# Turning the delta rule's normalized outputs by VectorE blocks and DRAM instead of TensorE

## The chip, the cores and the metric

The program runs on one core of one Trainium2 chip. The metric is the device time of one execution in microseconds (us); below it the median of several runs is given, and one execution was also taken by the hardware profiler.

## What is computed

One layer of a hybrid decoder trunk on 2048 tokens of width 1024, preceded by 16 meta tokens, in float32. The input is RMS-normalized and multiplied by one wide matrix; its columns feed two groups. Group A is a gated DeltaNet of 8 heads of 128 channels; group B is a short gated convolution. Both are put side by side, multiplied by `w_out`, added to the input and normalized once more.

```python
h = rmsnorm(x, norm_g); p = h @ w_in
q, k, v = split(silu(causal_dwconv(p_qkv, dn_conv_w)))        # l2norm of q and k per head
def step(S, inp):                                             # per head, chunk after chunk
    v_new = u_c - w_c @ S
    o = qd_c @ S + qk_c @ v_new
    S = S * gl_c + kd_c.T @ v_new
    return S, o
o = rmsnorm(o, dn_out_g) * silu(dn_z)                         # per head of 128 channels
o_sc = sc_b * causal_dwconv(sc_c * sc_h, sc_conv_w) * silu(sc_z)
return rmsnorm(x + concat([o_dn, o_sc]) @ w_out, final_g)
```

The part that matters here is the last line but two: the scan leaves `o` with tokens on the partitions, the norm is taken along the channels, and the product with `w_out` wants channels on the partitions. So each piece of 128 tokens by 128 channels has to be turned.

## The kernel before, in words

The 2048 tokens go through in two halves of 1024 (`hf`). For each half the wide product runs as a list of jobs of 128 columns each, and each job in groups of up to 512 tokens. A float32 product is made of three passes with rounded parts (`hh`, `hl` of the activations, `wh`, `wl` of the weights): hh·wh, hl·wh and hh·wl, 24 matmuls to a group, into one of three PSUM buffers `mm`. ScalarE rounds a loaded weight tile `wr` to `wh`, VectorE makes `wl` of the difference (`split_w`, line 713), and only when the second half of `wl` is made is the next weight load issued into that buffer (`load_w`, line 707).

Beside this runs the delta rule of one head after another, 16 in all (8 heads in each half of the tokens), as generators that a planner (`Model`, `pump`) resumes between the matmuls. The planner keeps an estimate of each engine's time, and an operation is written into its engine's list when the estimate says that its inputs are there. So the order on TensorE (PE), VectorE (DVE), ScalarE (ACT) and GpSimd (POOL) is fixed when the program is built, and each of these engines works through its list in that order and waits where an input is late. All DMAs are issued by SyncE (SP), also in one fixed order; that order is set by a scheduler of the framework.

- `delta_front` (line 962) makes the masked products of a head and inverts its 32x32 blocks on VectorE by `substitution` (line 933): 31 pairs `prod`, `XT`. The blocks pass through DRAM on their way there (`nbd<-E`, then `nb<-nbd`), four small DMAs each way.
- `delta_back` (line 1110) merges the blocks, loads the decays `qd` from DRAM and turns keys, values and queries on TensorE (PSUM tag `ta`). `qd` has one buffer, which the scan reads up to its last chunk, so the load for the next head waits for TensorE.
- `delta_scan` (line 1290) goes through the 8 chunks of a head. For each chunk: TensorE makes `rec<-S,k`; VectorE makes `yy` from it; TensorE adds `o<-S,qd` to the output and makes `rec<-yy,W`; ScalarE makes `vn`; TensorE makes `rec<-vn,kd` and `o<-vn,P`; VectorE makes the next state `S`. After every 4 chunks ScalarE copies the outputs from PSUM `o` to `os`.
- `delta_out` (line 1340) takes each `os` (4 pieces of 128x128; 32 such outputs, two for each head). ScalarE sums the squares, GpSimd and VectorE make the scale `so`, VectorE multiplies `os` by it, TensorE turns the four pieces into PSUM (`rec<-ident,os`, lines 1363 to 1365), and VectorE multiplies them with the gain and the gate into `zs` (line 1369). A DMA stores `zs` to `mixd`, from which the last product loads its input.

In the text an output is named by its head (0 to 15) and by first or second half (`b4` 0 or 1). While the first half is being normalized and turned, the scan of the second four chunks goes on.

Line 118, which the profile gives for nearly all instructions, is the planner's helper; so the rows are told apart by tile names.

Of the kernel before, what the change touches and what calls it, by code (L numbers as in the profile page):

```python
# [29 lines left out]
class Model:  # L30
# [33 lines left out]
    def after(self, *aps, slot=None, eng=None, lag=0.0, least=0.02):  # L64

        t = self.free["PE"] + least
        for a in aps:
            t = max(t, self.ready.get(a.tensor.name, 0.0))
        if slot is not None:
            q = self.slots.get((id(slot[0]), slot[1]), ())  # L70
            if len(q) == self.bufs.get((id(slot[0]), slot[1])):
                t = max(t, self.used.get(q[0], 0.0))
        if eng is not None:
            t = max(t, self.free[eng] - lag)
        return t - self.free["PE"]
# [98 lines left out]
def hybrid_trunk(  # L174
# [22 lines left out]
    nbd = tc.dram_tile([2, 32, 32, 32], F32, name="nbd")  # L197
    xtd = tc.dram_tile([2, 32, 32, 32], F32, name="xtd")
    ged = tc.dram_tile([2, NH * 9, 128], F32, name="ged")
    nmd = tc.dram_tile([2, NM, NM], F32, name="nmd")  # L200
    gtd = tc.dram_tile([2, NH * 9, 128], F32, name="gtd")

# [110 lines left out]
    def vt(pool, shape, tag, **kw):  # L313
        t = pool.tile(shape, kw.pop("dt", F32), tag=tag, name=tag, **kw)
        return model.tile(pool, tag, kw.get("bufs", nbufs.get(id(pool), 1)), t)
# [202 lines left out]
    def normalize(i):  # L518

        xt = vt(dp, [128, NC, 128], "kd").rearrange("p c i -> p (c i)")  # L520
        nc.sync.dma_start(xt, xs[HALF + 128 * i :][:128])
        yield after(xt)
        st = statistics(xt, 128, vt(dp, [128, 1840], "gw", dt=BF16))
        gains = []
        yield from hold("Q", True)

        def gain(c2):
            gains.append(vt(dp, [128, NC, 64], "Q").rearrange("p c i -> p (c i)"))
            nc.sync.dma_start(gains[c2], norm_g[0, 512 * c2 : 512 * c2 + 512].partition_broadcast(128))

        gain(0)
        yield after(gains[0], st[1])
        rs = refine(st, 128)
        for c2 in range(2):
            xc = xt[:, 512 * c2 : 512 * c2 + 512]
            nc.vector.scalar_tensor_tensor(xc, xc, rs, gains[c2], op0=ALU.mult, op1=ALU.mult)
            if c2 == 0:
                gain(1)
                yield after(gains[1])
        held.discard("Q")  # L540
        nc.sync.dma_start(xnd[i], xt)
        done.add(("xn", i))
# [28 lines left out]
    def hold(tag="ta", keep=False):  # L571
# [3 lines left out]
        if keep:  # L575
            held.add(tag)

    G = {}

    def gates(hf):  # L580
# [18 lines left out]
        yield after(abT, slot=(pta, "ta"))  # L599
        yield from hold()  # L600
        pt = ptile(pta, "ta", [128, 512])
        gw = vt(dp, [128, 920], "gw")
        ab2 = gw[:, 0:288].rearrange("p (c m) -> p c m", m=32)
        for c in range(NC):
# [78 lines left out]
        yield 3.5  # L683
        nc.scalar.activation(gT[:Wd], gT[:Wd], AF.Exp)
        nc.sync.dma_start(ged[hf, :Wd], gT[:Wd])
        G[hf] = dict(beta=beta, gcum=gcum, neg=neg, nch=nch)
        yield 2.0
        done.add(("G", hf))
# [121 lines left out]
    slot = {}  # L810
# [529 lines left out]
    def delta_out():  # L1340

        for _ in range(4 * NH):
            while not outputs:
                yield 0.3
            i, b4, os_, sq = outputs[0]
            hf, hd = divmod(i, NH)
            cs = slice(4 * b4, 4 * b4 + 4)
            mo, so, py, ptm = (vt(dp, [128, 4], a) for a in ("mo", "so", "opy", "opt"))
            yield after(os_)
            for c in range(4):  # L1350
                nc.scalar.activation(junk[:, 0:128], os_[:, c, :], AF.Square, accum_out=mo[:, c : c + 1])
            yield after(mo, eng="DVE", lag=0.3)
            nc.vector.scalar_tensor_tensor(mo, mo, 1.0 / HD, sq[:, cs], op0=ALU.mult, op1=ALU.add)
            power(py, mo, 4)
            yield after(py, eng="DVE", lag=0.3)
            newton(so, mo, py, ptm)
            nc.vector.tensor_tensor(
                out=os_, in0=os_, in1=so.unsqueeze(2).to_broadcast([128, 4, 128]), op=ALU.mult
            )
            while ("z", i) not in done:  # L1360
                yield 0.3
            yield after(os_, slot=(prec, "rec"))
            pt = ptile(prec, "rec", [128, 4, 128])
            for c in range(4):
                tr(pt[:, c, :], os_[:, c, :])
            outputs.popleft()
            ms = slice(512 * b4, 512 * b4 + 512)
            zs = slot[i]["zs"]
            nc.vector.scalar_tensor_tensor(
                zs[:, ms], pt.rearrange("p c i -> p (c i)"), dng, zs[:, ms], op0=ALU.mult, op1=ALU.mult  # L1370
            )
            t0 = hf * NC + 4 * b4
            nc.sync.dma_start(
                mixd[t0 : t0 + 4, :, hd, :].rearrange("t p j -> p t j"),
                zs[:, ms].rearrange("p (t j) -> p t j", j=128),
            )
            if b4 == 1:
                done.add(("out", i))
            yield 0.3

    STEP = 1.0
    SUBST = 0.8
    BACKLOG = 3
# [253 lines left out]
```

## Time and profile before

| | |
|---|---|
| median of 3 runs | 2236.77 us (2235.26 to 2238.23) |
| the profiled execution, its own time | 2236.26 us |
| its span from first to last instruction | 2234.5 us |
| PE busy | 2174.5 us, 97% |
| DVE busy | 1451.7 us, 65% |
| ACT busy | 854.0 us, 38% |
| POOL busy | 189.3 us, 8% |
| packets of the DMA queue that SP feeds, share of 16 engines | 46.0% |

Busy time is time in which an instruction was running; overlapping ones count once. The time outside the span is 1.8 us. In the rows further down, the name of an instruction is out<-in by the program's tile names, "xN" is the number of instructions, and a bracket at the end of a row gives the idle time of the engine before it and what ended it.

### The profile page before, as it was taken

To read this page: it belongs to the slowest core of one execution; us is meant where nothing else is said; L and a number is where in the kernel's file an instruction comes from. 1 tells how busy PE (TensorE), PEld (TensorE's weight loads), DVE (VectorE), ACT (ScalarE), POOL (GpSimd) and SP (SyncE) were. 2 spreads that over 40 slices of the span, in tenths; PEclk is the share of its full clock that TensorE was granted. 3 is DMA by queue.
4 is the path that set the end of the run, shared out by engine and by line. 5 is a ranking of instruction groups with operands and counts; after the bars stand their busy time and mean duration, and the time that the engine had idled before them with its cause. 6 is when DMAs were issued, how large, how long until landed. Compare 5 with 4: busy or idle time off the path is not lost.

```text
span 2234.5 us, 35464 instructions
## 1 busy us (share of the span) xinstructions
PE 2174.5 (97%) x13472; PEld 1917.1 (86%) x13472; DVE 1451.7 (65%) x3919; ACT 854.0 (38%) x1987; POOL 189.3 (8%) x345
## 2 busy tenths in 40 slices
PE   6999999999998999999999999999999999999998
PEld 6999999999998999977888888888888877888886
DVE  4677777677775668686767677676767674444422
ACT  5533434343443334444344352425252523332211
POOL 4010101010101010111010101010101000000000
PEclk9999999999999999999999999999999999999999
DMA  5434544353446744523444423343677343645521
GB/s 140 76 77 67 86 70 95 64 95 65 92 61 78 83 76 89 131 43 60 82 70 65 83 57 78 53 78 53 79 52 75 60 114 126 203 170 188 188 91 57
DMA packets 258537, 199.41 MB, mean 89 GB/s; under 512 B 62117, under 2 KB 226478, under 8 KB 258366
## 3 DMA queue, kind: packets, MB, share of 16 engines
q1 hardware_dynamic: 258366, 197.14, 46.0%
q8 instruction: 106, 1.74, 0.3%
q14 instruction: 65, 0.53, 0.1%
HBM read 160.51 MB, written 36.59 MB: 88 GB/s over the span
## 4 chain that ended last, share of the span: by engine, by line
PE 88%; DMA 4%; DVE 3%; ACT 2%; SPq 1%; issue 1%; POOL 0%; POOLq 0%; ACTq 0%; DVEq 0%
PE mm L118 75%; PE ta L118 7%; PE rec L118 4%; PE o L118 2%; DMA kd<-in_x_dram 2%; SPq L118 1%; ACT junk L118 1%; DMA wr<-in_w_in_dram 1%; DMA nb<-nbd 1%; DVE prod L118 1%; DMA xtd<-XT 0%; DVE wl L118 0%; DVE XT L118 0%; ACT wh L118 0%; DVE acc L118 0%
## 5 line engine op out<-in xcount | busy, mean ns | idle before, releaser
L118 PE MATMUL mm<-hh,wh 128*128 128x512 f32 (+3 forms) x2816 | 1008.4, 366 | 8.7 <-ACT hh L118 6.7
L118 PE MATMUL mm<-hl,wh 128*128 128x512 f32 (+3 forms) x2816 | 985.4, 357 | 0.4 <-DVE hl L118 0.4
L118 PE MATMUL mm<-hh,wl 128*128 128x512 f32 (+3 forms) x2816 | 640.1, 360 | 1.7 <-DVE wl L118 1.7
L118 PEld LDWEIGHTS mm<-hh,wh 128*128 128x128 f32 x2816 | 533.1, 190 | 60.3 <-ACT hh L118 7.9
L118 PEld LDWEIGHTS mm<-hl,wh 128*128 128x128 f32 x2816 | 532.5, 190 | 48.1 <-DVE hl L118 1.9
L118 PEld LDWEIGHTS mm<-hh,wl 128*128 128x128 f32 x2816 | 479.6, 189 | 48.9 <-DVE wl L118 2.2
L118 DVE TENSOR_TENSOR wl<-wr,wh 128x512 fp32r<-128x512 f32 x356 | 238.3, 689 | 97.6 <-ACT wh L118 77.0
L118 DVE SCALAR_TENSOR_TENSOR acc<-raw,pcol,acc 128x384 f32<-128x384 f32 (+2 forms) x360 | 232.9, 649 | 87.9 <-ACT acc L118 83.8
L118 ACT ACTIVATE wh<-wr 128x1024 fp32r<-128x1024 f32 x182 | 191.9, 1055 | 88.7 <-PE mm L118 49.7
L118 DVE SCALAR_TENSOR_TENSOR prod<-nb,XT 128x8 f32<-128x8 f32 (+30 forms) x496 | 191.0, 385 | 22.7 <-DMA nb<-nbd 19.1
L118 DVE TENSOR_REDUCE XT<-prod 128x8 f32<-128x16 f32 (+30 forms) x496 | 147.2, 297 | 17.0
L118 ACT ACTIVATE vn<-rec,cj 128x128 f32<-128x128 f32 x128 | 46.9, 366 | 248.4 <-PE rec L118 248.1
L118 ACT ACTIVATE raw<-mm 128x384 f32<-128x384 f32 (+2 forms) x120 | 61.5, 513 | 192.7 <-PE mm L118 192.2
L118 PE MATMUL mm<-oh,wh 128*128 128x512 f32 x256 | 101.9, 398 | 0.0
L118 ACT ACTIVATE sc_c<-mm 128x384 f32<-128x384 f32 (+3 forms) x82 | 42.1, 515 | 154.4 <-PE mm L118 154.3
L118 PE MATMUL mm<-ol,wh 128*128 128x512 f32 x256 | 100.4, 392 | 0.0
L118 DVE SCALAR_TENSOR_TENSOR yy<-rec,neg,vr 128x128 f32<-128x128 f32 x128 | 44.5, 348 | 56.1 <-PE rec L118 55.5
L118 DVE TENSOR_TENSOR y<-mm,y 128x512 f32<-128x512 f32 x21 | 14.5, 691 | 101.1 <-PE mm L118 101.1
L118 ACT ACTIVATE ojk<-y 128x512 bf16<-128x512 f32 x21 | 13.2, 631 | 164.6 <-DVE y L118 127.1
L118 DVE SCALAR_TENSOR_TENSOR S<-S,egl,rec 128x128 f32<-128x128 f32 x104 | 35.7, 343 | 59.6 <-PE rec L118 59.1
L118 POOL TENSOR_TENSOR opy<-mo,nhalf 128x4 f32<-128x4 f32 x32 | 34.3, 1073 | 460.3 <-DVE mo L118 451.5
L118 POOL TENSOR_SCALAR_AFFINE_SELECT E<-E 128x1024 f32<-128x1024 f32 x16 | 18.3, 1143 | 641.8 <-PE ta L118 352.3
(240 smaller groups left out, 2574.4 us busy)
## 6 DMA issues: line engine op xcount, KB each, us to landing
wr<-in_w_in_dram SPq DMA_DIRECT2D x128, 512.0 KB, 7.8
wr<-mixd SPq DMA_DIRECT2D x54, 512.0 KB, 4.3
E<-gtd SPq DMA_DIRECT2D x16, 512.0 KB, 3.8
qd<-ged SPq DMA_DIRECT2D x16, 512.0 KB, 6.4
nb<-nbd SPq DMA_DIRECT2D x64, 128.0 KB, 2.8
mixd<-zs SPq DMA_DIRECT2D x32, 256.0 KB, 2.4
out_dram<-y SPq DMA_DIRECT2D x16, 512.0 KB, 2.7
kd<-in_x_dram SPq DMA_DIRECT2D x9, 512.0 KB, 7.6
```

Of the source, the lines that this page charges most:

```text
L118: r = real(*args, **kw)
```

## The change

After the scale is applied, VectorE transposes the 32x32 blocks of all 128 partitions in one instruction into a buffer `gw`; four DMAs, one for each 32 partitions, write the blocks to their turned place in a DRAM tensor `osd`; one DMA reads the turned output back into the buffer `os`. TensorE's four transposes and their PSUM buffer are left out, and `zs` is made from `os` in SBUF. `gw` is shared with the gates and with the statistics of `normalize`, so holds are added there.

```diff
+    osd = tc.dram_tile([2, 4, 128, 128], F32, name="osd")
...
         yield after(xt)
+        yield from hold("gw")
         st = statistics(xt, 128, vt(dp, [128, 1840], "gw", dt=BF16))
...
+    def turn_out(dram, src, tmp):
+
+
+        nc.vector.transpose(out=tmp.rearrange("p c i -> p (c i)"), in_=src.rearrange("p c i -> p (c i)"))
+        for a in range(4):
+            nc.sync.dma_start(
+                dram[:, :, 32 * a : 32 * a + 32].rearrange("c (b y) x -> y (c b) x", b=4),
+                tmp[32 * a : 32 * a + 32].rearrange("y c (b x) -> y (c b) x", b=4),
+            )
...
         pt = ptile(pta, "ta", [128, 512])
+        yield from hold("gw", True)
         gw = vt(dp, [128, 920], "gw")
...
         nc.sync.dma_start(ged[hf, :Wd], gT[:Wd])
+        held.discard("gw")
...
+            yield after(slot=(dp, "gw"))
+            yield from hold("gw", True)
+            turn_out(osd[b4], os_, vt(dp, [128, 4, 128], "gw"))
+            pt = vt(dp, [128, 4, 128], "os")
+            nc.sync.dma_start(pt, osd[b4].rearrange("c p i -> p c i"))
+            yield DRAIN
+            held.discard("gw")
             while ("z", i) not in done:
                 yield 0.3
-            yield after(os_, slot=(prec, "rec"))
-            pt = ptile(prec, "rec", [128, 4, 128])
-            for c in range(4):
-                tr(pt[:, c, :], os_[:, c, :])
+            yield after(pt, eng="DVE", lag=0.3)
             outputs.popleft()
...
+    DRAIN = 4.0
```

Since the planner places everything anew, all lists shift a little. Three places are shown, at head 12, first half. On SP the list before has the store of `zs` ahead of the block transfers, and the load of `qd` for head 13 further down:

```order
L118 DMA mixd<-zs 128x4x128
L118 DMA nbd<-E 32x8x32 x4
L118 DMA nb<-nbd 32x1024 x4
L118 DMA wr<-in_w_in_dram 128x8x128
L118 DMA qd<-ged 128x1024
L118 DMA wr<-in_w_in_dram 128x8x128
L118 DMA mixd<-zs 128x4x128
```

and now the four writes to `osd`, two stores, that load of `qd`, and then the read of `os`:

```order
L118 DMA nb<-nbd 32x1024 x4
L118 DMA osd<-gw 32x16x32 x4
L118 DMA mixd<-sc_y 128x4x128 x2
L118 DMA qd<-ged 128x1024
L118 DMA os<-osd 128x4x128
L118 DMA mixd<-zs 128x4x128
L118 DMA wr<-in_w_in_dram 128x8x128
```

The way through DRAM has put five DMAs in, and `qd<-ged` now stands between the writes and the read.

On VectorE, `zs` of that output stood right behind the scaling of `os`, with one product of group B and one step of the scan between:

```order
L118 TENSOR_TENSOR os<-os,so 128x512
L118 TENSOR_TENSOR sc_u<-mm,sc_c 128x512
L118 SCALAR_TENSOR_TENSOR yy<-rec,neg_11238,vr 128x128
L118 SCALAR_TENSOR_TENSOR zs<-rec,pcol,zs 128x512
L118 TENSOR_TENSOR kpt<-kpy 128x8
```

Now it stands further down, between the state that chunk 6 leaves (`S`) and `yy` of chunk 7, the last of the head:

```order
L118 TENSOR_TENSOR sc_y<-sc_y,sc_c 128x512
L118 SCALAR_TENSOR_TENSOR prod<-nb,XT 128x8x4
L118 TENSOR_REDUCE XT<-prod 128x8
L118 SCALAR_TENSOR_TENSOR S<-S,egl,rec 128x128
L118 SCALAR_TENSOR_TENSOR prod<-nb,XT 128x8x5
L118 TENSOR_REDUCE XT<-prod 128x8
L118 SCALAR_TENSOR_TENSOR zs<-os,pcol,zs 128x512
L118 SCALAR_TENSOR_TENSOR yy<-rec,neg_11229,vr 128x128
L118 SCALAR_TENSOR_TENSOR prod<-nb,XT 128x8x6
```

From the block transpose to `zs` there are 17 instructions in the list of this output; over the 32 outputs it is 6 to 35. On TensorE the four transposes of this output stood among the matmuls of the wide product:

```order
L118 MATMUL mm<-hl,wh 128x512
L118 MATMUL rec<-ident,os 128x128 x4
L118 MATMUL mm<-hh,wh 128x512
L118 MATMUL mm<-hl,wh 128x512
L118 MATMUL rec<-yy,W 128x128
```

They are gone; the last chunk of head 12 now reads:

```order
L118 MATMUL rec<-S,k 128x128
L118 MATMUL o<-S,qd 128x128
L118 MATMUL mm<-hl,wh 128x512
L118 MATMUL mm<-hh,wh 128x512
L118 MATMUL mm<-hl,wh 128x512
L118 MATMUL mm<-hh,wh 128x512
L118 MATMUL mm<-hl,wh 128x512
L118 MATMUL rec<-yy,W 128x128
```

Five matmuls stand between the last use of `qd` and the matmul that needs `yy` of chunk 7.

## Rows read from the trace of the kernel before

**Rows 1.** The page: busy time; then its chain of waits by engine.
```profile
PE 2174.5 (97%) x13472; PEld 1917.1 (86%) x13472; DVE 1451.7 (65%) x3919; ACT 854.0 (38%) x1987; POOL 189.3 (8%) x345
...
PE 88%; DMA 4%; DVE 3%; ACT 2%; SPq 1%; issue 1%; POOL 0%; POOLq 0%; ACTq 0%; DVEq 0%
```

**Rows 2.** Groups by shape (count | busy us, mean ns | idle before, releaser): the transposes.
```profile
L118 PE MATMUL rec<-ident,os 128*128 128x128 f32 x128 | 19.4, 274 | 5.6 <-DVE os L118 5.6
```

**Rows 3.** Timeline of PE at one output: start us, us, what.
```profile
1078.88 0.39 PE L118 MATMUL mm<-hh,wl 128*128 128x512 f32 x1
1079.11 0.60 PE L118 MATMUL rec<-ident,os 128*128 128x128 f32 x4
1079.47 0.71 PE L118 MATMUL mm<-hh,wl 128*128 128x512 f32 x2
```

**Rows 4.** Timeline of PE at the longest wait for `os`.
```profile
724.75 0.66 PE L118 MATMUL rec<-ident,os 128*128 128x128 f32 x4 [3.79 <-DVE os L118]
```

**Rows 5.** Stretches after it: length, busy times, then PEclk, DMA share, GB/s.
```profile
726.00:728.00 2.00, 2.00 (x12) 2.00 (x11) 1.93 (x4) 1.79 (x4) 0.00 (x0) 0.51 0.77 186
728.00:730.00 2.00, 2.00 (x12) 2.00 (x12) 1.53 (x4) 0.00 (x0) 0.00 (x0) 0.64 0.09 28
```

**Rows 6.** Groups by shape on DVE: a transpose, the scaling, the gate.
```profile
L118 DVE STREAM_TRANSPOSE X<-W 32x256 f32<-32x256 f32 x48 | 20.7, 432 | 2.2 <-DMA W<-xtd 1.1
L118 DVE TENSOR_TENSOR os<-os,so 128x512 f32<-128x512 f32 x32 | 22.4, 700 | 1.1
L118 DVE SCALAR_TENSOR_TENSOR zs<-rec,pcol,zs 128x512 f32<-128x512 f32 x32 | 23.9, 748 | 13.1 <-PE rec L118 12.6
```

**Rows 7.** Timeline of SP: block transfers of head 9, no load between.
```profile
1156.18 1.81 SPq L118 DMA_DIRECT2D nbd<-E  x4
...
1159.31 1.71 SPq L118 DMA_DIRECT2D nb<-nbd  x4
```

**Rows 8.** DMA issues: KB each, median us from issue to landing.
```profile
wr<-in_w_in_dram SPq DMA_DIRECT2D x128, 512.0 KB, 7.8
qd<-ged SPq DMA_DIRECT2D x16, 512.0 KB, 6.4
mixd<-zs SPq DMA_DIRECT2D x32, 256.0 KB, 2.4
```

**Rows 9.** Stretches of the transfers in rows 7: writes, then reads (columns as rows 5).
```profile
1157.00:1158.00 1.00, 1.00 (x7) 0.87 (x6) 0.21 (x1) 0.07 (x1) 0.00 (x0) 1.00 0.45 66
1161.00:1162.00 1.00, 1.00 (x6) 0.80 (x5) 0.35 (x2) 0.76 (x4) 0.00 (x0) 1.00 0.92 275
```

**Rows 10.** Timeline of DVE: one `yy` of the scan.
```profile
1799.45 0.34 DVE L118 SCALAR_TENSOR_TENSOR yy<-rec,neg,vr 128x128 f32<-128x128 f32 x1
```

**Rows 11.** Timeline of SP, head 5: a weight load between write and read.
```profile
679.85 1.80 SPq L118 DMA_DIRECT2D nbd<-E  x4
681.76 0.39 SPq L118 DMA_DIRECT2D wr<-in_w_in_dram  x1
683.01 7.80 SPq L118 DMA_DIRECT2D nb<-nbd  x4
```

**Rows 12.** Timelines of DVE and PE: what waited for the reads, heads 5 and 15.
```profile
698.53 0.17 DVE L118 SCALAR_TENSOR_TENSOR prod<-nb,XT 128x8 f32<-128x8 f32 x1 [7.07 <-DMA nb<-nbd]
...
699.22 0.79 PE L118 MATMUL rec<-yy,W 128*128 128x128 f32 x2 [3.63 <-DVE yy L118]
...
1799.84 0.49 PE L118 MATMUL rec<-yy,W 128*128 128x128 f32 x2 [2.39 <-DVE yy L118]
```

**Rows 13.** The view of tile `nbd`: who waited for it (us, times).
```profile
  DVE prod L118: 19.1, 6
```

**Rows 14.** Timelines of DVE, SP and ACT at head 12, first half.
```profile
1568.63 0.69 DVE L118 TENSOR_TENSOR os<-os,so 128x512 f32<-128x512 f32 x1
...
1580.93 0.58 SPq L118 DMA_DIRECT2D qd<-ged  x1
...
1582.47 0.60 ACT L118 ACTIVATE os<-o 128x512 f32<-128x512 f32 x1 [0.96 <-PE o L118]
```

## The prediction

> **What bounds the kernel.** I read the busy times first, then the chain of waits, then the waits of PE, and last the lists of SP and DVE beside the timeline. PE is busy for 97% of the span and makes 88% of the chain that ends last; DVE is busy for 65% [rows 1]. So what is taken from PE shortens the kernel, what is added on DVE or in a DMA costs nothing while PE has its inputs in time, and a wait of DVE costs as soon as PE runs into it. The profiled execution took 2236.26 us, 0.5 us under the median of the three runs; the sum below is made on 2236.3 and needs no correction for the median. A measurement of this kernel can tell about 0.2%, 4.5 us, from no change.
>
> **What is removed.** 128 transposes on PE, four for each of 32 outputs. Their mean duration is 274 ns [rows 2], but PE overlaps them with their neighbours: four of them start at 1079.11 and the next matmul at 1079.47, against 0.23 us from one matmul to the next around them [rows 3]. They hold PE for 0.36 us an output, 32 x 0.36 = **11.5 us**. The Trainium skill (TensorE: Matmul & The Clock Gate, Part 4: PE-mode transpose) gives about 275 ns for such a transpose in a kernel; counted in full that would free 35.2 us and turn the sum below into 2227. The trace's starts decide for 0.36 us.
>
> PE also waited 5.6 us for `os` [rows 2], of which 3.79 us in one piece [rows 4]; **5.6 us** go. Behind that piece the granted clock was 0.51 for 2 us and 0.64 for the next 2 [rows 5]: the lower of the two levels for part of them, (0.49 + 0.36) x 2 = **1.7 us** lost, which go too. Gain: 18.8 us.
>
> **What is added on DVE.** 32 block transposes of 128x512. The trace has such a transpose only at 32x256, 432 ns; the elementwise scaling at 128x512 takes 700 ns [rows 6]. If all partitions go side by side, as in every elementwise row, it is 0.7 us each, 22 us in all; if the four groups of 32 partitions went one after another, 4 x 0.8 = 3.2 us each, 102 us. I take 0.7, the row of the same shape. DVE has 35% idle, and only outputs beside a running scan make PE wait for it: **1 us** (0 to 10). `zs` keeps its shape and reads SBUF instead of PSUM; 748 ns [rows 6] stay.
>
> **What is added on SP and the DMA engines.** Five DMAs an output. The nearest row is the way of the 32x32 blocks: four writes issued within 1.8 us, then four reads that SP can issue 3.1 us after the first write [rows 7]. The new writes hold twice as many pieces of 128 bytes, so about 4 us; one read of 256 KB adds some 2.4 us, the landing time of `mixd<-zs` with its equal size [rows 8]. Without company the trip takes 6.5 to 7 us. The pieces are small but not slow: in the stretch of the writes 66 GB/s took a share of 0.45, in that of the long reads 275 took 0.92 [rows 9], half the rate for each share.
>
> **The wait that comes in.** `zs` now waits on DVE for the read of `os`, and everything behind it on DVE waits along. From the block transpose to `zs` the new list holds 17 instructions at head 12, mostly of 0.2 to 0.7 us, such as `yy` and the scaling [rows 6, 10]. With the idle time of DVE that covers most of a trip without company. But in the new SP list 31 of the 32 outputs have another DMA between the writes and the read, mostly a 512 KB weight load or the `qd` load; the second half of head 6 alone has none. The trace shows what that does: with a weight load issued at 681.76 between write and read, the data was there at 698.53, DVE stood 7.07 us and PE 3.63 us [rows 11, 12]. The reads came out behind the load. All six waits of DVE for these block reads make 19.1 us [rows 13], and all six are heads with a weight load between; PE lost 3.63 + 2.39 = 6.0 us in two of them [rows 12].
>
> How much PE loses depends on what stands behind `zs`. In seven first-half outputs (heads 0, 5, 9, 11, 12, 13 and 14) it is `yy` of the last chunk, which PE needs within a few matmuls. I price these apart.
>
> - *Heads 12 and 14.* Here `qd<-ged` stands ahead of the read. It may only be issued when PE has used `qd` for the last time; in the trace before, at this head, 1580.93, 1.5 us before the next copy of `os`, and 12.3 us after the scaling of the first one began [rows 14]. In the new list of DVE the state `S` that this last use needs has only two or three small instructions between it and `zs`. So DVE reaches `zs` while `qd` has just been allowed out: 0.4 us to issue, 6.4 us to land [rows 8], 0.7 us for the read behind it, then `zs` 0.75 and `yy` 0.34 [rows 6, 10]: `yy` is ready 8.6 us after the last use of `qd`. PE arrives at its matmul after five others, 5 x 0.23 = 1.15 us [rows 3]. It waits 7.5 us.
> - *Head 11.* A weight load stands ahead of the read, and it waits for the second half of `wl`, which DVE makes three instructions ahead of `zs`. 7.8 us to land [rows 8] and 0.7 for the read, less the 0.4 us of DVE work between: a wait of 8 us, of which PE sees about 7.5.
> - *Heads 0, 5, 9, 13.* The same, but 5 to 8 us of DVE work, more with DVE's idle time, lie between `wl` and `zs`: hidden.
>
> So three waits of 7.5 us, and after each the clock is low as it was behind 3.79 us [rows 5], 1.7 us more: 3 x 9.2 = **27.6 us**. From below this is some 9 us (3 us each, if the loads land twice as fast and the clock holds); from above 3 x (16.8 - 1.15 + 1.7) = 52 us, with the 16.8 us from load to data of head 5 [rows 11, 12]. I take the median landings, since nothing marks these three loads as slow.
>
> - *The other 29 outputs.* Behind their `zs` stand the substitution, convolutions, `wl`, or a last state that is only needed half a kernel later; PE meets these later, and its three `mm` buffers cover some. Below 0. Above, if each of the 25 that are not hidden as just told cost what the six heads cost on average, 6.0 us and two low clocks of 1.7 [rows 12, 5], (6.0 + 3.4) / 6 = 1.6 us each, 39 us. I take **5 us**, near the lower end, since four of the six cost nothing.
>
> **Sum.** 2236.3 - 11.5 - 5.6 - 1.7 + 1 + 27.6 + 5 = **2251 us**: the transposes leave PE, but the trip through DRAM hangs behind other loads on SP's one queue, and three times PE waits for it.
>
> **The rivals.**
> - *Faster: the trip fits under the DVE work.* If the `qd` and weight loads drain in 2 to 3 us, as the reads of head 9 did [rows 7, 9], the data is there when DVE arrives at `zs`. It decides at heads 11, 12 and 14: a read that lands within about 2 us of the last use of `qd`. For it speak ten of the sixteen block trips, which made DVE wait nowhere [rows 13]; against it the landings of 6.4 and 7.8 us. 2236.3 - 18.8 + 3 = 2221. Chance 0.16.
> - *Faster: the whole duration of a transpose is freed.* If the overlap in [rows 3] were made by the records alone, 128 x 0.274 = 35.1 us go instead of 11.5: 2227. Chance 0.04.
> - *No change.* One or two of the three places pay, 9 or 18 us, and the rest is hidden: 2228 to 2240, most of it around 2236. Chance 0.15.
> - *Much slower: the waits spread.* The other outputs cost 1.6 us each, or the 160 added DMAs push the block transfers of `delta_front` and the weights late: 2251 + 25 = 2276. Against it: four of the six heads in that row cost PE nothing, and SP issues a DMA in 0.4 to 0.5 us [rows 7]. Chance 0.17.
> - *The turned writes crawl.* If the turned writes ran at 15 GB/s instead of the 66 of the block writes [rows 9], 256 KB would take 17 us instead of 4, and each output would be 13 us later; with PE losing 6.0 of every 19.1 us that DVE waits [rows 12, 13], 32 x 13 x 0.31 = 129 us more: 2380. The Trainium skill (VectorE: DVE Perf Modes, The three transpose paths) warns that a plain DMA which transposes by its strides is 19 times slower than the crossbar; of the 275 GB/s above, an estimate by it would leave 14. Here the pieces are 128 bytes long and already turned inside, and [rows 9] speak against it. Chance 0.03.
>
> **How the numbers follow.** The forecast itself, 2243 to 2265, has 0.45. Faster by over 0.2% is 0.16 + 0.04 = 0.20, within 0.2% 0.15, slower 0.45 + 0.17 + 0.03 = 0.65. The lower ends of all terms give 2236.3 - 18.8 + 0 + 9 + 0 = 2226.5, the upper ends 2236.3 - 18.8 + 10 + 52 + 39 = 2318, which would need all of them at once. The range is 2226 to 2276: it leaves out about 0.1 of the faster cases below, and above half of the spreading waits and the crawl, another 0.1. Since both signs hold much of it, the forecast's own range stands beside it: 2243 to 2265.
>
> **What would show it right or wrong.** In the profile after, PE should have no `rec<-ident,os`, and 128 instructions fewer. DVE should have 32 transposes near 0.7 us. DVE should wait for `os<-osd` for some 50 to 100 us over the outputs; PE should wait for `yy` near 25 us in all, with its longest waits at heads 11, 12 and 14 and a low clock behind each. It is wrong if DVE waits for `os<-osd` under 20 us, if PE's waits for `yy` stay under 12 us, or if the loss sits in the waits of `mm` or `ta`.

## The result, and the profile after

| | median | runs | ratio to before, 95% interval |
|---|---|---|---|
| before | 2236.3 us | 2235.3 to 2238.2 | |
| the change | 2359.7 us | 2355.5 to 2362.2 | 1.0549 [1.0530, 1.0567] |

The change is slower by 123 us, 5.5%; the prediction had 2251 and a range of 2226 to 2276. The direction was right, the size was not.

The profiled execution has a span of 2353.7 us (before 2234.5). Its page, busy times, chain by engine and one line of the groups:

```profile
PE 2204.0 (94%) x13344; PEld 1935.6 (82%) x13344; DVE 1453.9 (62%) x3955; ACT 854.5 (36%) x1989; POOL 186.2 (8%) x345
...
PE 68%; DMA 15%; DVE 11%; ACT 3%; SPq 2%; issue 1%; POOLq 0%; POOL 0%; DVEq 0%; ACTq 0%
...
L118 DVE SCALAR_TENSOR_TENSOR zs<-os,pcol,zs 128x512 f32<-128x512 f32 x32 | 24.0, 750 | 129.7 <-DMA os<-osd 129.5
```

Beside [rows 1], 128 instructions have left PE, yet PE is busy for 29.5 us longer and, span less busy time, idle for 149.7 us instead of 60.0. The chain's share of PE fell from 88% to 68%, and that of DMA rose from 4% to 15%. `zs`, which waited 13.1 us in [rows 6], now waits 129.5 us for its read. That PE is busy longer with less to do goes with a lower mean granted clock over the span (view of the cores: span, clock). It was 0.992 before, and is now:

```profile
core 0: 2353.7 us, clock 0.968
```

By the trace's clock records it is at 0.50, the lower of its two levels (1.2 GHz), in 24 stretches, 154 us together; before it was in 8, 36 us. The block transposes are as forecast (x count | busy, mean ns | idle before), and the writes land fast, but the reads don't (us from issue to landing, median):

```profile
L118 DVE STREAM_TRANSPOSE gw<-os 128x512 f32<-128x512 f32 x32 | 22.7, 710 | 4.2 <-ACT gw L118 3.1
```

```profile
nb<-nbd SPq DMA_DIRECT2D x64, 128.0 KB, 6.3
osd<-gw SPq DMA_DIRECT2D x128, 64.0 KB, 2.0
os<-osd SPq DMA_DIRECT2D x32, 256.0 KB, 7.5
```

Who waits is seen in PE's waits (us in total, times, longest):

```profile
PE rec L118 <- DVE yy L118: 41.2, 10, 11.0
PE mm L118 <- DVE wl L118: 13.8, 6, 7.9
PE ta L118 <- DVE vr L118: 11.5, 6, 6.0
PE mm L118 <- DVE sc_u L118: 11.0, 2, 8.5
PE ta L118 <- ACT kd L118: 8.6, 3, 4.0
PE rec L118 <- DVE S L118: 8.0, 5, 5.0
```

`yy` was foreseen; the others are the work of other parts of the program. Which of these waits come from `zs` is told below, by a run with the same lists in which `zs` does not wait. Two places show both kinds. First head 11, first half, one of the three in the prediction: timelines of SP, VectorE and PE, then stretches (length, busy times, PEclk, DMA share, GB/s):

```profile
1548.99 0.37 SPq L118 DMA_DIRECT2D wr<-in_w_in_dram  x1
1549.54 0.45 SPq L118 DMA_DIRECT2D os<-osd  x1
```

```profile
1560.75 0.75 DVE L118 SCALAR_TENSOR_TENSOR zs<-os,pcol,zs 128x512 f32<-128x512 f32 x1 [11.47 <-DMA os<-osd]
1561.79 0.34 DVE L118 SCALAR_TENSOR_TENSOR yy<-rec,neg,vr 128x128 f32<-128x128 f32 x1
```

```profile
1562.18 0.80 PE L118 MATMUL rec<-yy,W 128*128 128x128 f32 x2 [11.03 <-DVE yy L118]
```

```profile
1556.00:1562.00 6.00, 0.00 (x0) 0.00 (x0) 1.22 (x4) 0.00 (x0) 0.00 (x0) 0.54 0.33 89
1562.00:1568.00 6.00, 5.82 (x18) 4.83 (x19) 4.22 (x15) 2.61 (x11) 0.00 (x0) 0.61 0.16 45
```

The weight load goes out at 1548.99, the read 0.55 us behind it, and `zs` starts 11.8 us after that load. PE stands 11.03 us, and then runs 6 us at a mean clock of 0.61.

Second head 12, second half, one of the 29 outputs that the prediction priced at 5 us together:

```profile
1703.59 0.39 SPq L118 DMA_DIRECT2D wr<-in_w_in_dram  x1
1704.16 0.44 SPq L118 DMA_DIRECT2D os<-osd  x1
```

```profile
1717.50 0.75 DVE L118 SCALAR_TENSOR_TENSOR zs<-os,pcol,zs 128x512 f32<-128x512 f32 x1 [6.75 <-DMA os<-osd]
...
1734.61 0.68 DVE L118 TENSOR_TENSOR vr<-ta,ir 128x512 f32<-128x512 f32 x1
```

```profile
1735.34 1.12 PE L118 MATMUL ta<-ident,q 128*128 128x128 f32 x4 [6.04 <-DVE vr L118]
```

No `yy` stands here. VectorE waits 6.75 us for the read and then works for 17 us without a pause until it comes to `vr`. `vr` reads a `ta` buffer, and until it has done so PE has no buffer for its next transposes of inputs: it stands 6.04 us.

### The profile page after: what moved, and what is told of

Read it like the earlier page. It is cut to its first block, busy times and chain, and to the rows that moved or that the text cites. A ratio compares the mean times of both kernels' runs of the same rounds, so it can differ in the third digit from the quotient of the medians.

```text
span 2353.7 us, 35518 instructions
## 1 busy us (share of the span) xinstructions
PE 2204.0 (94%) x13344; PEld 1935.6 (82%) x13344; DVE 1453.9 (62%) x3955; ACT 854.5 (36%) x1989; POOL 186.2 (8%) x345
## 4 chain that ended last, share of the span: by engine, by line
PE 68%; DMA 15%; DVE 11%; ACT 3%; SPq 2%; issue 1%; POOLq 0%; POOL 0%; DVEq 0%; ACTq 0%
PE mm L118 56%; DMA os<-osd 8%; PE ta L118 6%; PE rec L118 3%; DVE acc L118 2%; SPq L118 2%; DVE prod L118 2%; DMA wr<-in_w_in_dram 2%; PE o L118 2%; DVE wl L118 1%; DVE XT L118 1%; DMA Q<-in_norm_g_dram 1%; DMA osd<-gw 1%; DMA nmd<-mM 1%; ACT junk L118 1%
## 5 line engine op out<-in xcount | busy, mean ns | idle before, releaser
L118 PE MATMUL mm<-hl,wh 128*128 128x512 f32 (+3 forms) x2816 | 997.5, 362 | 1.5 <-DVE hl L118 1.5
L118 PE MATMUL mm<-hh,wl 128*128 128x512 f32 (+3 forms) x2816 | 651.8, 365 | 14.0 <-DVE wl L118 13.8
L118 PEld LDWEIGHTS mm<-hh,wh 128*128 128x128 f32 x2816 | 541.9, 193 | 78.3 <-issue 17.2
L118 PEld LDWEIGHTS mm<-hl,wh 128*128 128x128 f32 x2816 | 541.7, 193 | 49.3 <-DVE hl L118 2.2
L118 PEld LDWEIGHTS mm<-hh,wl 128*128 128x128 f32 x2816 | 489.5, 193 | 64.9 <-DVE wl L118 18.0
L118 DVE SCALAR_TENSOR_TENSOR zs<-os,pcol,zs 128x512 f32<-128x512 f32 x32 | 24.0, 750 | 129.7 <-DMA os<-osd 129.5
L118 PE MATMUL rec<-yy,W 128*128 128x128 f32 x256 | 52.8, 289 | 41.2 <-DVE yy L118 41.2
L118 PEld LDWEIGHTS rec<-yy,W 128*128 128x128 f32 x256 | 47.2, 197 | 51.2 <-DVE yy L118 45.9
```

Of the source, the lines that this page charges most:

```text
L118: r = real(*args, **kw)
```

## The experiments

All ratios are to the kernel before, run on the same chip. "Four lists" are the lists of PE, VectorE, ScalarE and GpSimd; where they are called those of the change or of before, they are equal instruction for instruction. Where `zs` reads `os` or `gw` without the read from DRAM, the turn is left out, and the outputs of that run are not those of the program; it serves for the time alone.

### What takes the time: transposes, order, DMAs, wait

First the parts alone. In each of these the planner made its own lists.

**Only VectorE's transposes**, added to the kernel before (`spare` is not read):

```diff
...
+            spare = vt(dp, [128, 4, 128], "gw")
+            nc.vector.transpose(out=spare.rearrange("p c i -> p (c i)"), in_=os_.rearrange("p c i -> p (c i)"))
...
```

> The kernel before with only VectorE's 32 block transposes added, into a buffer nobody reads. Theory 1 and 2: 32 x 0.7 us on an engine that is 65% busy, 2236 to 2240. Theory 3 (the transposes on VectorE cost the time): over 2290.

2235.2 us, 0.9991 [0.9977, 1.0004]: no loss shows, and theory 3 is out for the transposes. That they cost nothing is not shown, for the planner's new lists have also taken something away: VectorE's waits for `nb<-nbd` are 3.1 us here instead of the 19.1 of [rows 13]. A run further down takes these waits out of the kernel before by themselves and stands at 2227.0, so up to some 8 us of the transposes or of the new lists may be hidden here.

**The whole trip, unread**, added to the kernel before:

```diff
...
+            turn_out(osd[b4], os_, vt(dp, [128, 4, 128], "gw"))
+            spare = vt(dp, [128, 4, 128], "gw")
+            nc.sync.dma_start(spare, osd[b4].rearrange("c p i -> p c i"))
...
```

> The kernel before, with its transposes on PE and zs from PSUM, and with the whole trip added beside it: block transpose into gw, four writes, and a read back into gw that nothing uses. Theory 1 (the wait of zs): nothing waits for the read, so 2236 plus at most a few us for VectorE, 2236 to 2245. Theory 2 (the DMAs make nb, wr and qd late): more than half of PE's gaps in the changed kernel, 63.8 of 118.4 us, lie away from a zs; with the low clock behind them that is some 70 us, 2300 to 2320. A value between them would divide the loss.

2250.2 us, 1.0065 [1.0048, 1.0083]: 15 us between this and the last one, a value between theories 1 and 2: so the company of 160 DMAs is a part of the loss, but a small one.

**The change without its trip**, `zs` from `gw`:

```diff
-            turn_out(osd[b4], os_, vt(dp, [128, 4, 128], "gw"))
-            pt = vt(dp, [128, 4, 128], "os")
-            nc.sync.dma_start(pt, osd[b4].rearrange("c p i -> p c i"))
+            pt = vt(dp, [128, 4, 128], "gw")
+            nc.vector.transpose(out=pt.rearrange("p c i -> p (c i)"), in_=os_.rearrange("p c i -> p (c i)"))
...
```

> The change without its way through DRAM: VectorE transposes the 32x32 blocks, and zs reads them as they lie in gw, so the blocks are not carried to their turned places; no osd DMAs. Theory 1 (zs stands in VectorE's list and waits for a late read): the loss and the transposes on PE are both gone, 2236.3 - 18.8 + 1 = 2218, say 2214 to 2226. Theory 2 (the 160 added DMAs make other transfers late, whoever reads them): the same, 2218. Theory 3 (VectorE's transposes, or the new order of its list, cost the time): still over 2300.

2248.0 us, 1.0051 [1.0035, 1.0068]. A miss for all theories: most of the loss is gone, but the transposes that PE no longer makes do not show. So the next three runs fix the lists and take away one thing at a time. The planner is told of the instruction that is left out (`planned`), so that it writes the same lists.

**Before's lists without the 128 transposes:**

```diff
-                tr(pt[:, c, :], os_[:, c, :])
+                planned("tensor", "transpose", [pt[:, c, :]], [os_[:, c, :], ident])
...
-                zs[:, ms], pt.rearrange("p c i -> p (c i)"), dng, zs[:, ms], op0=ALU.mult, op1=ALU.mult
+                zs[:, ms], os_.rearrange("p c i -> p (c i)"), dng, zs[:, ms], op0=ALU.mult, op1=ALU.mult
```

> The kernel before with its lists as they are, but without the 128 transposes on PE; zs reads the scaled os as it lies, so the turn is left out. This is the removed work alone, without the planner's answer to it. If PE's time is freed as the prediction's sum has it: 2236.3 - 11.5, and most of the 5.6 and 1.7 of PE's waits for os, 2218 to 2226. If PE's freed time is given back in waits whatever the order: 2232 to 2240.

2228.2 us, 0.9963 [0.9952, 0.9975], between the two, nearer to the first.

**The change's lists without its DMAs**, `zs` from `os`, the writes and the read only planned:

```diff
-            nc.sync.dma_start(
+            planned("sync", "dma_start",
...
-            nc.sync.dma_start(pt, osd[b4].rearrange("c p i -> p c i"))
+            planned("sync", "dma_start", [pt], [back])
```

> The same lists on the four engines, zs again from the scaled os, and none of the 160 DMAs to and from osd. The turn is left out. If the new order of the lists costs nothing: 2236.3 - 18.8 + 1 = 2218, 2214 to 2226. If the order costs as in the kernel without the trip: 2240 to 2255. The distance to the kernel that issues the DMAs unread is what the DMAs cost by company alone: 15 us by the unread trip beside the kernel before.

2251.3 us, 1.0068 [1.0050, 1.0087]: the order costs.

**The change's lists with the DMAs, but nobody waits for the read:**

```diff
-            nc.sync.dma_start(pt, osd[b4].rearrange("c p i -> p c i"))
+            tc.nc.sync.dma_start(tmp, back)
...
-                zs[:, ms], pt.rearrange("p c i -> p (c i)"), dng, zs[:, ms], op0=ALU.mult, op1=ALU.mult
+                zs[:, ms], os_.rearrange("p c i -> p (c i)"), dng, zs[:, ms], op0=ALU.mult, op1=ALU.mult
```

> The lists of PE, VectorE, ScalarE and GpSimd are those of the change, instruction for instruction, and the five DMAs of each output are issued; but zs reads the scaled os as it lies, and the read from osd goes back into gw, where nobody uses it. So the turn is left out, and only the wait is taken away. Theory 1 (the wait of zs in VectorE's list, with the low clock behind it, is the loss): about 95 us of the 123 come back, 2255 to 2275, what stays being what the unread trip cost beside the kernel before (15 us) and the new order (some 10 us, as without the trip). Theory 2 (the DMAs delay other transfers): under 40 us come back, 2320 or more.

2271.5 us, 1.0155 [1.0136, 1.0173]. (SP's list, which the framework makes, differs in a few places from the change's.) This gives the loss in four steps, each a difference of two medians; PE busy and idle (span less busy) are differences of their pages:

| step | time | PE busy | PE idle |
|---|---|---|---|
| 2237.4 to 2228.2: the transposes leave PE | -9 us | -12.7 | +4.6 |
| to 2251.3: the new order of the lists, VectorE's transposes | +23 us | +11.2 | +9.4 |
| to 2271.5: the 160 DMAs, unread | +20 us | +3.3 | +15.5 |
| to 2359.7: `zs` waits for the read | +88 us | +27.7 | +60.2 |

Along the last two steps the four lists are the same, so what PE is busy longer is its clock: 28 of the 88 us of the wait. The wait is the greater part of the loss; theory 1 stands.

The last two runs also show whom the wait reaches. PE's waits in the run in which nobody waits for the read:

```profile
PE rec L118 <- DVE yy L118: 11.7, 6, 6.4
PE mm L118 <- DVE sc_u L118: 10.3, 1, 10.3
PE rec L118 <- DVE S L118: 7.8, 5, 4.8
PE mm L118 <- DVE wl L118: 4.1, 4, 1.8
PE ta L118 <- DVE vr L118: 3.2, 3, 1.3
PE ta L118 <- ACT kd L118: 0.4, 1, 0.4
```

Against these, the change's waits for `yy`, `wl`, `vr` and `kd` have grown with the wait of `zs`; those for `sc_u` and `S` have not. The longest wait of `zs` shows why a wait is not yet a cost. At head 4, second half, the change has

```profile
783.39 0.75 DVE L118 SCALAR_TENSOR_TENSOR zs<-os,pcol,zs 128x512 f32<-128x512 f32 x1 [13.57 <-DMA os<-osd]
...
787.31 0.55 PE L118 MATMUL mm<-hh,wh 128*128 128x256 f32 x1 [8.47 <-DVE sc_u L118]
```

and with nobody waiting for the read VectorE waits as long for something else that stands ten instructions further down, a value `pxy` that GpSimd makes, and PE waits for `sc_u` all the same:

```profile
767.71 0.16 DVE L118 TENSOR_TENSOR pxt<-pxy 128x1 f32<-128x1 f32 x1 [13.32 <-POOL pxy L118]
...
770.68 0.69 PE L118 MATMUL mm<-hh,wh 128*128 128x384 f32 x1 [10.32 <-DVE sc_u L118]
```

With the matmuls of both runs put side by side one by one, the change falls behind by 88 us in all: by 13.4, 6.7 and 9.8 us around `zs` of heads 11, 12 and 14 (first halves), 29.9 together; by some 11 us at heads 0, 5, 9 and 13; by nothing at head 4, second half; and by the other 47 us or so at the rest, 4.5 of it at head 12, second half.

### Why the read is late

**Another queue.** GpSimd issues the five DMAs of each output:

```diff
+        self.own = _Engine(nc.gpsimd, "DMA", model)
...
-            nc.sync.dma_start(
+            nc.own.dma_start(
...
-            nc.sync.dma_start(pt, osd[b4].rearrange("c p i -> p c i"))
+            nc.own.dma_start(pt, osd[b4].rearrange("c p i -> p c i"))
```

> The change with the five DMAs of each output issued by GpSimd (8% busy) instead of SP; the lists of PE, VectorE and ScalarE are those of the change. Theory 1a (the read stands behind weight and qd loads in SP's one queue): the read is issued as soon as the writes have landed and is back some 6 to 8 us after the block transpose; VectorE's waits for os<-osd fall from 129.5 us to under 50, time 2270 to 2300. Theory 1b (the DMA engines themselves are busy with those loads, whichever queue the read comes from): the reads still take 7 us and more, the waits stay over 100 us, time 2330 to 2370.

2376.4 us, 1.0627 [1.0611, 1.0644], slower than the change and outside both expectations. The reads were freed, as theory 1a said: landing and VectorE's waits for them. But a new wait took their place:

```profile
os<-osd POOLq DMA_DIRECT2D x32, 256.0 KB, 3.4
```

```profile
DVE XT L118 <- POOL prod L118: 129.1, 15, 12.7
...
DVE zs L118 <- DMA os<-osd: 34.8, 12, 7.0
```

GpSimd issues the read only when the writes have landed, and stands until then (138 us in all in its waits); behind it in its list stand the masks for `prod`, which VectorE's substitution needs.

**SP in the order of the program**, so that reads follow their writes directly; the same for the kernel before, and for a version with a later `zs` that comes below:

```diff
                 mybir.EngineType.Pool,
+                mybir.EngineType.SP,
```

> The change with SP's list in the order of the program too: the read of os stands directly behind its four writes, and the block reads directly behind theirs, in all heads; the lists of the four engines are those of the change. If the loads that stood between write and read made the wait: VectorE's waits for os<-osd fall from 129.5 us to under 50, those for nb<-nbd from 40.9 to under 15, and the time to 2245 to 2290. If the reads are late because the DMA engines still work at loads issued before the writes, or because SP now stands at the writes while other loads wait behind it: waits over 100 us or a new wait for wr, and 2320 to 2370.

> The kernel before, its four lists unchanged, with SP's list in the order of the program. Its block reads waited 19.1 us, from six heads with a weight load between. If the same holds there: those waits fall to a few us, 2224 to 2234. If SP's order by the program makes other loads late: 2236 to 2260, and the same cost is then in the change with this order.

2452.3 us, 1.0960 [1.0939, 1.0981], and for the kernel before 2373.9 us, 1.0611 [1.0592, 1.0629]. The local half came true, the waits for the reads are nearly gone, but the order costs the kernel before 137 us too, and both times lie outside all that was expected. VectorE's waits, then ScalarE's, of the change with this order:

```profile
DVE E L118 <- DMA E<-gtd: 144.4, 16, 16.6
...
DVE zs L118 <- DMA os<-osd: 12.9, 5, 5.4
```

```profile
ACT wh L118 <- DMA wr<-mixd: 193.0, 27, 12.4
```

In the change these were 2.1 us for `E` and 12.4 for `wr<-mixd`. By its list SP now stands before each DMA whose data or buffer is not ready, and loads that could have gone out (`E`, `wr` of the last product) wait behind it. The later `zs` with this order took 2464.1 us, where 2225 to 2255 was expected. So the order as a whole is no mend.

**Only weight and `qd` loads held behind the read** (the load of `qd` is wrapped like that of `J.wr`); the rest of SP's list stays the scheduler's:

```diff
+    def behind():
+        return tc.issue_after(getattr(last[-1], "ins", last[-1])) if last else contextlib.nullcontext()
...
-            nc.sync.dma_start(J.wr, win[:, :, J.col : J.col + 128])
+            with behind():
+                nc.sync.dma_start(J.wr, win[:, :, J.col : J.col + 128])
...
-            nc.sync.dma_start(pt, osd[b4].rearrange("c p i -> p c i"))
+            last.append(nc.sync.dma_start(pt, osd[b4].rearrange("c p i -> p c i")))
```

> The change, its four lists unchanged, and on SP only this: a weight load or a qd load that the program has after a read of os may not be issued ahead of that read. So no such load stands between write and read any more, while the rest of SP's list is the scheduler's. If the loads between made the wait: VectorE's waits for os<-osd fall from 129.5 us to under 60 and the time from 2360 to 2270 to 2310; what stays over the unread trip (2271) is the trip's own 7 us against the place of zs. If holding the loads back costs as much, as the order of the program did: 2340 or more.

2263.4 us, 1.0114 [1.0095, 1.0133], a little better than expected: 96 us come back, with the four lists of the change, the same trip and the same place of `zs`. Landing of the read, and VectorE's wait:

```profile
os<-osd SPq DMA_DIRECT2D x32, 256.0 KB, 2.8
```

```profile
DVE zs L118 <- DMA os<-osd: 9.8, 4, 4.3
```

From 129.5 us to 9.8. This settles it: the wait is made by the loads that stand between write and read on SP. The time is also 8 us under that of the run in which nobody waits (2271.5), so holding the loads back takes away a little beside the wait; what that is was not tried.

**A later `zs`** instead: a generator of its own makes `zs` after `LATE` us of planned time, and the read goes into `gw`, so that `os` is free early. 12 us, then 20:

```diff
...
+            outputs.popleft()
+            pt = vt(dp, [128, 4, 128], "gw")
             nc.sync.dma_start(pt, osd[b4].rearrange("c p i -> p c i"))
-            yield DRAIN
+            start(gate_out(i, b4, pt))
...
+    LATE = 12.0
```

> The change with zs at least 12 us of planned time behind the issue of the read instead of 4, in a generator of its own; the read goes back into gw, so os is free for the next copy as soon as it is transposed. Theory 1 (the wait of zs): the read has mostly landed when VectorE comes to zs; its waits for os<-osd fall from 129.5 us to under 40, and the time to 2218 to 2245. Theory 2 (the DMAs make nb, wr and qd late): PE's gaps away from zs stay, 2290 to 2320.

> As the kernel with zs 12 us of planned time behind the read's issue, which took 2295 and still waited 109.8 us on VectorE for the reads; now 20 us. Theory 1: the waits fall under 40 us and the time to 2245 to 2265, near the unread trip beside the kernel before (2250). If the time stays at 2285 to 2300, the rest of that loss is not the wait of zs.

2295.1 us, 1.0267 [1.0237, 1.0296], with 109.8 us of VectorE's waits left, far over the 40 expected, and a time in the range of theory 2; and 2258.4 us, 1.0098 [1.0081, 1.0115], with 3.7 us, which speaks for theory 1 again. So 12 us of planned time are not enough, 20 us are, and the time comes out 5 us below the hold on the loads, on lists that the planner has made anew.

### The same hazard in the kernel before, and what stays

The older trip, `nbd` and `nb`, has the same hazard. The hold was put on the block reads in the kernel before (`last.append` at `nb<-nbd`), in the change's lists without DMAs, in before's lists without transposes, and together with the hold on `os` in the change and in the version with the later `zs`.

> The kernel before, four lists unchanged, with weight and qd loads held behind the last block read in the same way. Six heads had a load between, and VectorE waited 19.1 us, PE 6.0 us in two of them with the low clock behind. If the place of the read on SP sets that: the waits fall under 5 us and the time to 2222 to 2233. If held loads come late for the next product: 2236 to 2250.

2227.0 us, 0.9947 [0.9932, 0.9962], **faster than both kernels**, as expected. VectorE's waits for `nb<-nbd`, 19.1 us in [rows 13], are gone, and PE's for `yy`, 7.5 us in the kernel before, are

```profile
PE rec L118 <- DVE yy L118: 1.5, 1, 1.5
```

> The lists of the change without the 160 DMAs (2251, which leaves out the turn), with weight and qd loads held behind the block reads: it had nine heads with a load between and 38.9 us of waits for nb<-nbd, against 19.1 in the kernel before. If these waits are why the 12 us that PE was given did not show: they fall under 10 us and the time to 2222 to 2238. If the order of the four lists is the cause: 2246 to 2256.

2244.2 us, 1.0027 [1.0015, 1.0038], between the two expectations. The waits for `nb<-nbd` fell from 38.9 to 1.7 us, the time by 7: the hazard is a part of the new order's cost, not all of it.

> The change, its four lists unchanged, with weight and qd loads held behind both the reads of os and the block reads: the same mend as in the kernel before that took 2227, and the one that took the change to 2263 with its 38.5 us of waits for nb<-nbd left. If those waits cost here what they cost the kernel before (10 us) and the trip-less lists (7 us): 2250 to 2258, some 27 us over the mended kernel before. If the two holds get in each other's way: 2263 or more.

2254.4 us, 1.0073 [1.0051, 1.0095], as expected.

> The change with zs 20 us of planned time behind the read (2258), and weight and qd loads held behind both kinds of reads. 17.3 us of waits for nb<-nbd and 9.4 for W<-xtd were left. 2240 to 2256 if those waits for nb<-nbd fall and nothing else grows; 2258 or more if the held loads come late.

2249.9 us, 1.0050 [1.0033, 1.0067], as expected; the best version that turns through DRAM, and still slower than before.

> The mended kernel before (2227) without the 128 transposes, its lists as they are, turn left out. If the removed work is worth what it is in the sum: 2208 to 2216, and then the distance to the change's lists with the same mend and no trip (2244) is the cost of the new order, about 30 us. If not: 2222 to 2228.

2215.6 us, 0.9903 [0.9887, 0.9918]: 11 us under the mended kernel before, at the upper edge of what was expected. With all reads mended, then, the removed transposes are worth 11 us (2227.0 to 2215.6), the new order costs 29 (to 2244.2), and trip and wait 10 (to 2254.4).

What the 29 us are is shown in part. The lists differ in order and by VectorE's transposes, whose own share is not known apart. The pages of the two give PE busy +16.2 us and idle +12.3 for the same work on PE. One stretch of the new order, columns as above:

```profile
1642.00:1648.00 6.00, 1.31 (x8) 0.84 (x8) 5.22 (x8) 5.91 (x14) 1.68 (x2) 0.98 1.01 47
1648.00:1654.00 6.00, 5.13 (x15) 3.61 (x15) 1.12 (x2) 5.49 (x20) 0.00 (x0) 0.50 0.51 55
1654.00:1660.00 6.00, 5.28 (x90) 4.42 (x90) 3.79 (x8) 0.77 (x3) 0.00 (x0) 0.50 0.91 48
1660.00:1666.00 6.00, 6.00 (x25) 4.28 (x25) 2.19 (x9) 1.67 (x4) 0.00 (x0) 0.50 1.00 45
1666.00:1672.00 6.00, 6.00 (x32) 5.36 (x32) 1.31 (x4) 0.59 (x1) 0.00 (x0) 0.53 0.33 91
```

and the same place in before's lists without the transposes:

```profile
1618.00:1624.00 6.00, 5.93 (x30) 4.54 (x29) 2.17 (x3) 5.86 (x17) 1.65 (x2) 1.00 0.98 54
1624.00:1648.00 24.00, 23.32 (x209) 18.86 (x208) 15.48 (x30) 13.55 (x26) 0.19 (x1) 1.00 0.59 56
```

In the new order PE was busy for 1.31 of 6 us where `delta_back` turns the inputs of a head, and some 24 us at the lower level followed. In the old order PE was busy for 5.93 of 6 us, and the clock is 1.00. That is 12 us of the 29 in this execution, at half the clock for 24 us. PE's lists differ here: in the new one six groups of `delta_back`'s transposes (`ta<-ident,k`, `vT` and `q`, each twice) follow one another with no matmul of the wide product between, and PE waits 1.29, 0.43 and 3.69 us among them for VectorE and ScalarE; in the old one matmuls of the product stand between any two groups. Why the planner places them so, and where the rest of the 29 us lies, stays open.

## Why the prediction was wrong

- **The work removed** was sized well where it was worked out by starts: 11.5 us for the transposes, and PE is busy for 12.7 us less on equal lists. Of the 7.3 us for waits on `os` and their clock little came: on equal lists the time falls by 9 (11 with the mend) instead of 18.8, since PE is idle for 4.6 us longer, not shorter. The rival in which the whole 274 ns of a transpose are freed, 35 us, is out. The Trainium skill (TensorE: Matmul & The Clock Gate, Part 4: PE-mode transpose) gives about 275 ns for one in a kernel; the rows have that duration too, and it is no price of a transpose that stands among others.
- **VectorE's transposes**: 0.7 us each was forecast, 710 ns measured. That they cost 1 us is not contradicted, but not shown either: with them alone the time stays, on lists in which another wait is gone.
- **The trip**: writes land in 2.0 us and the read, when no load is let out ahead of it, in 2.8. At head 6, second half, the one output with nothing between, SP issues the read 3.5 us after the first write; with 2.8 for landing that is 6.3 us, an estimate near the 6.5 to 7 of the prediction. The crawl is out.
- **The mechanism**: right. Loads ahead of the read in SP's queue make `zs` late. The Trainium skill (DMA: Bandwidth & Descriptors, Queues, rings and completion order) says that each DMA engine takes the descriptors of one ring in their order; the 7.5 us against 2.8 agree.
- **The three places** at heads 11, 12 and 14 were priced at 27.6 us, three equal waits of 7.5 and their clock. PE's gaps behind these `zs` are 11.0, 5.0 and 8.1, and with the clock the change falls behind by 29.9 us there. That the sum comes out is partly luck: one place was half as long again as forecast, another two thirds.
- **The step that failed** is "the other 29 outputs, 5 us", with its reasons that four are hidden and that PE meets what stands behind the `zs` of the rest later, with three `mm` buffers to cover some. Of the 88 us that the wait costs on equal lists, some 58 lie at these 29 outputs: some 11 at the four called hidden (heads 0, 5, 9 and 13) and some 47 at the others. VectorE waited 129.5 us, not 50 to 100, at 24 outputs, and only 26.5 of it at the three places. Behind the other waits stood `yy`, `wl`, `vr` and, on ScalarE, `kd`, and PE did meet them. The upper bound of 39 us was worked out from the six waits of [rows 13], 3.2 us each, of which PE lost 0.31 us for each us that VectorE waited. Here a wait has 5.4 us on average (129.5 / 24), and PE was idle for 0.46 us to each (60.2 / 129.5), its clock not counted.
- **The clock** was priced at 1.7 us behind each of three waits. On equal lists the wait made PE busy for 28 us longer.
- **Two terms were missing**: "all lists shift a little", said ahead of the prediction, had no price and cost 23 us, VectorE's transposes included; the company of the 160 DMAs stood only in a rival and cost 20.
- **A sum is off**: the rival in which the waits spread adds 25 us for 1.6 us at each of the other outputs. At its own 25 outputs that is 39 us, 34 more than the 5 in the sum, so 2285 and not 2276. The measured time lies far above both.
- **The tests named** did not all go as forecast: PE's waits for `yy` are 41.2 us instead of 25. The longest are at heads 11 and 14; the next, 6.5 us ahead of `zs` of head 12, is there without the wait of `zs` too (6.4) and comes from a late block read. And a large part of the loss sits where it was said that it would show the prediction wrong, in waits for `mm` and `ta` buffers and inputs.

## What to carry to other kernels

Before a value is sent through DRAM, read what stands between its write and its read in the issuing engine's list: a 512 KB load there made a read of 2.8 us take 7.5, and holding the loads back gave 96 of 123 us. An engine that works in order hands such a wait to everything behind the reader, so price the whole list behind it, and the same when the issue is moved to another engine. What a wait in a profile costs is known when a run takes it away on the same lists: the longest one here, 13.6 us, cost nothing, because another as long stood behind it. In a planned kernel a removed instruction changes every list: measure the removed work on the old lists before crediting it.

## What was not expected of the hardware

One and the same kind of load ran at very different speeds. A weight load has 512 KB in pieces of 512 bytes. With the weight load at head 4 and the read of `os` behind it in flight, both in such pieces, all DMA engines were busy at some 50 GB/s (share 1.02 and 1.04):

```profile
772.00:776.00 4.00, 4.00 (x25) 4.00 (x24) 0.00 (x0) 0.00 (x0) 0.00 (x0) 1.00 1.02 47
776.00:780.00 4.00, 2.84 (x17) 2.52 (x15) 0.00 (x0) 0.00 (x0) 0.00 (x0) 1.00 1.04 56
```

A weight load alone, in the mended kernel before, moved two to three times as much:

```profile
1341.00:1342.00 1.00, 1.00 (x8) 0.92 (x8) 0.81 (x3) 0.72 (x2) 0.00 (x0) 1.00 0.97 147
1342.00:1343.00 1.00, 1.00 (x8) 0.82 (x6) 0.96 (x7) 0.00 (x0) 0.00 (x0) 1.00 0.77 129
```

By the trace's packets one piece took 145 ns in the median in the first place and 27 in the second. It is not the second DMA that makes the difference: in the kernel before, a weight load issued at 1648.41, with the next DMA only at 1657.83 and no other packets in this stretch, was as slow, 154 ns to a piece:

```profile
1652.00:1656.00 4.00, 4.00 (x21) 3.33 (x20) 2.26 (x3) 2.90 (x5) 0.00 (x0) 1.00 1.02 51
```

So how late a read comes behind a load also depends on how fast the load itself runs. What makes the packets slow was not tried.
